# Two-layer FoX/NSA trunk on one core: the z sections of layer 0 three head pairs later

## The chip, the core and the metric

The kernel runs on one core of a Trainium2 chip. The metric is device time in microseconds (us) for one launch. A core has a matrix engine (PE, with its weight loads shown apart as PEld), a vector engine (DVE), a scalar engine (ACT), a general engine (POOL) and a queue engine (SP), which issues all DMAs of this kernel. Each engine works off its own list of instructions in order.

## What is computed

Two layers act on x of 1024 tokens by 1024 channels. Layer 0 is forgetting attention with 16 heads of 64 channels, layer 1 is sparse attention. The change touches layer 0 alone. Cut to that:

```python
h = rmsnorm(x, norm_g[0])
q, k, v, f, z = split(h @ w_in)           # 1024 channels each, f 16
c = cumsum(log_sigmoid(f + b_f))
logits = q k^T / 8 + c[query] - c[key]    # causal, per head
o = softmax(logits) v
x = x + (o * silu(z)) @ w_out
```

## The kernel before, in words

**Units of work.** Heads go in pairs p = 0 to 7; a pair is 128 channels. A *section* is the projection of h to 128 channels of k, v, q or z: two halves of 512 tokens, and for each half eight *triples* (`mm3`, L132 to L135: three matmuls of 512 columns that build one float32 product out of high and low parts). So a section is 16 triples. `load_w` (L123) brings a section's weights by DMA, DVE makes the high part (L128) and POOL the low part (L129); `next_w` loads one section ahead.

**Attention** of a pair is eight *duos* (`FoxDuo`, L538 on). A duo is `score` (S matmuls L579 and L580, three chunks; DVE adds the bias and finds the minimum, L588; ACT exp, L597, and copy, L598; DVE low part, L599; a transposing DMA to `pT`, L600), and, two duos later, `pv` (L613, L614) and `finish` (small DVE work, L622 to L627). After the eighth duo of a pair `finish` transposes the pair's output (`pto`, L635, two groups of four), multiplies it by silu(z) on DVE (L637) and stores it in DRAM as rows of `oF` (L638). The S chunks have three PSUM buffers (`psS`, L50).

**Order.** `merge` (L208) writes the attention (`fox_main`, L653) and the sections (`fox_fill`, L438) into one order: after each step of a duo (its scores, its pv) it takes triples from the fill until their written costs (650 a triple) come up to `ratio` times the written costs of the attention so far. `PACE` is 2.3, and 2.6 (`LAST`) from the eighth pair on. The last triple may overshoot, and with `rebase` an overshoot is not given back. A step may wait for a mark in `ready`: the attention of pair p waits for q of p; k of pair p waits in the fill until all scores of pair p - 2 are written, and v of p until its last `finish`. While the fill waits so, attention steps follow one another without triples, and the triples owed are written in one run when the mark is there. The framework keeps this order on each engine, and draws a later instruction ahead where it reckons that an earlier one would wait.

**Fill.** The sections stand in the order z0 k1 v1 q1 z1 k2 ... (k0 v0 q0 come before the attention). For pair 7 they are split: half of q7, half of z7, `load_wout` of half the output weights (DMA, ACT copy L530, POOL subtraction L531), then the other halves. Behind that stands `out_start` (L464): triples `y` of the output projection of token tiles 4, 5 and 6 with rows 0 to 3, then 4 to 6 of `oF` as far as pairs 0 to 6 go, and row 7 at the end. `out_layer` (L673) does the other five tiles, and layer 1 follows.

Of the kernel before, what the change touches and what calls it, by code (L numbers as in the profile page):

```python
# [8 lines left out]
F32 = mybir.dt.float32  # L9
# [4 lines left out]
AF = mybir.ActivationFunctionType  # L14
OP = mybir.AluOpType
# [4 lines left out]
D = 1024  # L20
S = 1024
P = 128
# [13 lines left out]
def f(ap):  # L36
    return ap.bitcast(F32)
# [3 lines left out]
def tile_fox_nsa(ctx, tc, a, out):  # L41
    nc = tc.nc
    V, A, G, T = nc.vector, nc.scalar, nc.gpsimd, nc.tensor
    dma = nc.sync.dma_start
# [3 lines left out]
    dram = ctx.enter_context(tc.tile_pool(name="dram", bufs=1, space=DRAM))  # L48
# [13 lines left out]
    def ps_a(name):  # L62
        return psA.tile([P, 512], F32, tag="A", name=name)
# [14 lines left out]
    ready = {}  # L78

    def silu2(dst, src):  # L80

        A.activation(dst, src, AF.Tanh, scale=0.5)
        V.scalar_tensor_tensor(dst, dst, 1.0, src, OP.add, OP.mult)
# [168 lines left out]
    oF = dram.tile([D, S], F32, name="oF")  # L252
# [3 lines left out]
    hp = tc.alloc_tile_pool(name="hT0", bufs=1, side="right")  # L256
    st = tc.alloc_tile_pool(name="start", bufs=1, side="right")
    sa = tc.alloc_tile_pool(name="sa", bufs=2)
# [2 lines left out]
    def wsec(kind, p):  # L261
        return load_w(wp, a["fox_w"][kind * 8 + p], f"{'qkvz'[kind]}{p}")

    fox_order = [x for p in range(8) for x in ((1, p), (2, p), (0, p), (3, p))][1:]
    wq = []

    def next_w(take=True):
        while len(wq) < 2 and fox_order:
            wq.append(wsec(*fox_order.pop(0)))
        return wq.pop(0) if take else None  # L270
# [51 lines left out]
    sb = []  # L322
# [94 lines left out]
    def fox_q(p, w, halves=(1, 0)):  # L417
        Q = ready.setdefault(("qt", p), {})
        for half in halves:
            pt = ps_a(f"q{p}_{half}")  # L420
            yield from project(w, hT, half, pt)
            for j in range(2):
                Q[half, j] = q = sa.tile([P, 512], F32R, tag="Q", bufs=8, name=f"Q_{p}_{half}_{j}")
                r, o = rows[j], rows[1 - j]
                A.activation(q[r, :], pt[r, :], AF.Copy, scale=-SCALE)
                V.scalar_tensor_tensor(q[o, :], pt[r, :], -SCALE, f(q[r, :]), OP.mult, OP.subtract)
            ready["q", p, half] = Q

    def fox_z(p, w, halves=(1, 0)):
        zs = ready.setdefault(("zt", p), {})  # L430
        for half in halves:
            pt = ps_a(f"z{p}_{half}")
            yield from project(w, hT, half, pt)
            zs[half] = z = sb[0].tile([P, 512], F32, tag="z", bufs=4, name=f"z_{p}_{half}")
            silu2(z, pt)
            ready["z", p, half] = zs

    def fox_fill():  # L438
        for p in range(8):
            if p >= 2:  # L440
                yield lambda p=p: ("scored", p - 2) in ready
            yield from k0 if p == 0 else fox_k(p)
            if p == 0:
                for _ in range(11):
                    yield next(gate0)
            if p >= 2:
                yield lambda p=p: ("done", p - 2) in ready
            yield from fox_v(p)
            if p == 0:
                yield from gate0  # L450
                sb.append(tc.alloc_tile_pool(name="sb", bufs=2, reuse_waits="tile"))
            wo_copy(0, p)
            if p < 7:
                yield from fox_q(p, next_w())
                yield from fox_z(p, next_w())
            else:
                wq, wz = next_w(), next_w()
                for half in (1, 0):
                    yield from fox_q(p, wq, (half,))
                    yield from fox_z(p, wz, (half,))  # L460
                    yield from load_wout(hp, 0, half)
        yield from out_start()

    def out_start():  # L464


        ys = ready["ys"] = {}
        ws = {}

        def split(t, c, src):  # L470
            oh, ol = ws[t]
            A.copy(oh[:, c, :], src)
            V.tensor_tensor(ol[:, c, :], src, f(oh[:, c, :]), OP.subtract)

        def rows_of(t, c):
            yield lambda: ("o", c.stop - 1, 1) in ready
            of = wp.tile([P, KC, P], F32, tag="wst", bufs=1, name=f"of0{t}_{c.start}")
            dma(of[:, c, :], oF[c.start * P:c.stop * P, t * P:(t + 1) * P].rearrange("(k p) t -> p k t", p=P))
            split(t, c, of[:, c, :])

        def products(t, c):
            oh, ol = ws[t]
            for half in range(2):
                for k in range(c.start, c.stop):
                    wh, wl = ready["wout"][k // 4]
                    cs = slice(half * 512, half * 512 + 512)
                    mm3(ys[t][half], oh[:, k, :], ol[:, k, :], wh[:, k % 4, cs], wl[:, k % 4, cs], k == 0, k == KC - 1)
                    yield 650

        for t, banks in ((4, (ps_a, ps_s)), (5, (ps_a, ps_t))):  # L490
            ws[t] = out_parts(f"0{t}")
            ys[t] = [ps(f"y0_{t}_{half}") for half, ps in enumerate(banks)]
            yield from rows_of(t, slice(0, 4))
            yield from products(t, slice(0, 4))
        for t in (4, 5):
            yield from rows_of(t, slice(4, 7))
        ws[6] = [sa.tile([P, S], F32R, tag=x, bufs=4, name=f"o06_{x}").rearrange("p (k t) -> p k t", k=KC) for x in ("KH", "KL")]
        yield from rows_of(6, slice(0, 7))
        for t in (4, 5):
            yield from products(t, slice(4, 7))  # L500
        yield lambda: "scores" in ready
        ys[6] = [ps_s(f"y0_6_{half}") for half in range(2)]
        yield from products(6, slice(0, 7))
        yield lambda: ("o", 7, 1) in ready
        for t in (4, 5, 6):
            split(t, slice(7, 8), ready["z", 7, 1][1][:, (t - 4) * P:(t - 3) * P].rearrange("p (k t) -> p k t", k=1))
        for t in (4, 5, 6):
            yield from products(t, slice(7, 8))

# [23 lines left out]
        ready.setdefault("wout", []).append((hi, lo))  # L533


    PACE, LAST = 2.3, 2.6

    class FoxDuo:  # L538

# [77 lines left out]
        def finish(self):  # L617
            p, j, x, lr = self.p, self.j, self.x, self.lr
            if j == x == 0:
                self.O[p] = sb[0].tile([P, NT, P], F32, tag="o", bufs=1, name=f"o_{p}")  # L620
            o = self.O[p]
            V.tensor_tensor(lr[:, 1:2], lr[:, 1:2], lr[:, 2:3], OP.add)  # L622
            V.reciprocal(lr[:, 4:6], lr[:, 0:2])
            t = sb[0].tile([P, 2, 64], F32, tag="ot", bufs=2, name=f"ot_{self.name}")
            V.tensor_reduce(t, self.po.rearrange("p (u c) -> p u c", u=2)[:, :, 0:128].rearrange("p u (c d) -> p u d c", c=2),
                            AX.X, OP.add)
            V.tensor_tensor(o[:, 3 - x:5 + x:2 * x + 1, 64 * j:64 * j + 64], t, lr[:, 4:6, None].to_broadcast([P, 2, 64]), OP.mult)  # L627
            if j == 1 and x == 3:
                ready["done", p] = True
                for s in (1, 0):  # L630
                    yield lambda s=s: ("z", p, s) in ready
                    yield 1000
                    pt = ps_t(f"pto_{p}_{s}")
                    for i in range(4):
                        T.transpose(pt[:, i * P:(i + 1) * P], o[:, 4 * s + i, :], ident)  # L635
                    z = ready["z", p, s][s]
                    V.scalar_tensor_tensor(z, pt, ready["v", p][1], z, OP.mult, OP.mult)  # L637
                    dma(oF[p * P:(p + 1) * P, s * 512:(s + 1) * 512], z)  # L638
                    ready["o", p, s] = True
                    yield 450  # L640

    def burst(gens):
# [10 lines left out]
    def fox_main():  # L653
        duos = [FoxDuo(p, j, x) for p in range(8) for j in range(2) for x in range(4)]
        for n in range(len(duos) + 2):
            if n == len(duos) - 8:
                yield (LAST,)
            if n < len(duos):
                yield from burst(duos[n].score(u) for u in (1, 0))
                if duos[n].j == 1 and duos[n].x == 3:  # L660
                    ready["scored", duos[n].p] = True
                    if duos[n].p == 7:
                        ready["scores"] = True
            if n >= 2:
                yield from burst(duos[n - 2].pv(u) for u in (0, 1))
                yield from duos[n - 2].finish()

    merge(fox_main(), fox_fill(), PACE, rebase=True)
    sb[0].release()
    sa.release()  # L670

# [81 lines left out]
    nq, wq = list(nsa_w), []  # L753
# [446 lines left out]
    for qi in range(4):  # L1200
        n = P * (qi + 5)
# [262 lines left out]
```

## Time and profile before

| | us |
|---|---|
| median of 3 runs | 1553.28 |
| those runs | 1551.80 to 1553.96 |
| profiled execution, its time | 1553.53 |
| profiled execution, span from first to last instruction | 1551.7 |

The span is 1.83 us shorter than the time of the same execution. In the rows of stretches further down the columns are: from:to, length in us, busy us of PE, PEld, DVE, ACT and POOL, each with "(x90)" for 90 instructions, then the TensorE clock that was granted (1.00 is 2.4 GHz, 0.50 is 1.2 GHz), the mean busy share of the 16 DMA engines and GB/s. In rows in order of time the first two numbers are start and duration in us. A bracket such as `[2.19 <-DVE m L588]` gives the idle time of the engine before the instruction and what ended it. Layer 0's attention lies between about 72 and 585 us of the span.

### The profile page before, as it was taken

Reading aid. Unit: us, or ns where it says so; the run is one execution under the profiler, and the core shown is the slowest. Engines: PE = TensorE matmul, PEld = TensorE weight load, DVE = VectorE, ACT = ScalarE, POOL = GpSimd, SP = SyncE. Lnnn points to the kernel's source line nnn. Section 1 sums busy time; section 2 is a strip of 40 time slices with the busy share of each in tenths; the row PEclk is TensorE's granted clock in tenths of the full one; section 3 lists DMA queues with packets and bytes.
Section 4 is the critical chain, followed back from the end, with each engine's and each line's share of the span. In section 5 each row is a group of like instructions: output and inputs, shape, how many; then the busy total and the mean of one; then the engine's idle time right before and its main releaser. Section 6 shows DMA issues by size and latency. Waiting matters only on the chain.

```text
span 1551.7 us, 29460 instructions
## 1 busy us (share of the span) xinstructions
PE 1434.4 (92%) x10488; PEld 1188.4 (77%) x10488; DVE 1063.7 (69%) x2756; ACT 803.3 (52%) x2025; POOL 556.5 (36%) x604
## 2 busy tenths in 40 slices
PE   5999999999999787999999979899898998888898
PEld 4888888888787666878888768687787877667686
DVE  6586878778787755457364687787686777678433
ACT  5364646545555643233133655566565666567321
POOL 1232323222233500043241342557647657345300
PEclk9999999999999889999999999999999999899899
DMA  7796767867878756343345586757756856674642
GB/s 263 223 183 146 163 155 156 172 160 149 178 156 174 166 104 231 95 133 96 126 134 176 149 202 179 206 123 151 168 122 143 195 118 137 151 167 113 161 138 95
DMA packets 405763, 242.72 MB, mean 156 GB/s; under 512 B 332464, under 2 KB 353840, under 8 KB 405360
## 3 DMA queue, kind: packets, MB, share of 16 engines
q1 hardware_dynamic: 405616, 240.84, 63.5%
q8 instruction: 83, 1.36, 0.4%
q14 instruction: 64, 0.52, 0.1%
HBM read 120.96 MB, written 44.11 MB: 106 GB/s over the span
## 4 chain that ended last, share of the span: by engine, by line
PE 61%; DVE 16%; ACT 6%; DMA 6%; POOL 6%; issue 4%; SPq 1%; POOLq 0%; DVEq 0%; ACTq 0%
PE S_n L1256 4%; DVE P_n L1263 3%; PE y L133 3%; PE y L135 3%; PE y L134 3%; POOL hl_n L1270 3%; PE ptp_n L1288 2%; PE v L133 2%; PE v L135 2%; PE v L134 2%; PE S L579 2%; PE S L580 2%; PE q L133 2%; PE O L613 2%; PE k L133 2%
## 5 line engine op out<-in xcount | busy, mean ns | idle before, releaser
L1266 ACT ACTIVATE P_n<-P_n,m_n 128x640 f32<-128x640 f32 (+7 forms) x256 | 187.0, 731 | 74.6 <-DVE m_n L1265 37.3
L1256 PE MATMUL S_n<-nk,nq 128*128 128x320 f32 (+5 forms) x768 | 189.0, 356 | 19.4 <-DVE m_n L1263 18.6
L597 ACT ACTIVATE P<-P,m 128x512 f32<-128x512 f32 (+1 forms) x192 | 116.9, 610 | 133.2 <-DVE m L588 132.3
L568 POOL TENSOR_TENSOR Bd<-B,tri 128x128 f32<-128x128 f32 x128 | 62.3, 501 | 245.3 <-DVE m L588 228.5
L1263 DVE CUSTOM_DVE_ANT_0 P_n<-S_n,wmask 128x128 f32<-128x128 f32 (+1 forms) x192 | 113.5, 598 | 53.4 <-POOL hl_n L1270 37.7
L1256 PEld LDWEIGHTS S_n<-nk,nq 128*128 128x128 f32 x768 | 125.2, 194 | 32.3 <-DVE m_n L1263 23.3
L1270 POOL TENSOR_TENSOR hl_n<-P_n,hl_n 128x640 f16<-128x640 f32 (+4 forms) x128 | 141.5, 1109 | 7.5
L599 DVE SCALAR_TENSOR_TENSOR hl<-P,hl 128x512 f16<-128x512 f32 (+1 forms) x192 | 124.1, 664 | 21.8 <-ACT hl L598 20.7
L150 ACT ACTIVATE pth_n<-ptp_n 128x512 f16<-128x512 f32 (+1 forms) x160 | 86.6, 546 | 76.1 <-PE ptp_n L1288 75.4
L1288 PE MATMUL ptp_n<-ident,P_n 128*128 128x128 f32 x576 | 98.2, 292 | 19.3 <-DVE ptl_n L151 10.3
L151 DVE SCALAR_TENSOR_TENSOR ptl_n<-ptp_n,pth_n 128x512 f16<-128x512 f32 (+1 forms) x160 | 100.5, 634 | 20.8 <-ACT pth_n L150 20.1
L1269 POOL CAST hl_n<-P_n 128x640 f16<-128x640 f32 (+4 forms) x128 | 74.1, 584 | 98.7 <-ACT P_n L1266 78.4
L133 PE MATMUL y<-wo,ohi 128*128 128x512 f32 x240 | 96.8, 403 | 8.0 <-ACT ohi L693 8.0
L1288 PEld LDWEIGHTS ptp_n<-ident,P_n 128*128 128x128 f32 x576 | 71.3, 149 | 33.1 <-DVE ptl_n L151 11.9
L134 PE MATMUL y<-wo,ohi 128*128 128x512 f32 x240 | 96.0, 400 | 0.0
L135 PE MATMUL y<-wo,olo 128*128 128x512 f32 x240 | 94.9, 398 | 0.9 <-DVE olo L694 0.9
L598 ACT ACTIVATE hl<-P 128x512 f16<-128x512 f32 (+1 forms) x192 | 92.5, 513 | 4.3 <-DMA pT<-hl 2.8
L1296 PE MATMUL O_n<-nv,pth_n 128*128 128x64 f16 x576 | 76.1, 199 | 3.7 <-ACT pth_n L150 3.7
L579 PE MATMUL S<-KH,Q 128*128 128x512 f32 (+1 forms) x192 | 68.8, 372 | 10.6 <-DVE m L588 10.4
L1297 PE MATMUL O_n<-nv,pth_n 128*128 128x64 f16 x576 | 74.9, 197 | 0.0
L1298 PE MATMUL O_n<-nv,ptl_n 128*128 128x64 f16 x576 | 72.2, 197 | 0.0
L1296 PEld LDWEIGHTS <-pth_n 128*128 128x128 f16 x576 | 53.8, 101 | 21.4 <-ACT pth_n L150 9.1
(384 smaller groups left out, 4517.0 us busy)
## 6 DMA issues: line engine op xcount, KB each, us to landing
nq<-qD SPq DMA_DIRECT2D x64, 256.0 KB
B<-cD SPq DMA_DIRECT2D x16, 512.0 KB
wo<-wD SPq DMA_DIRECT2D x16, 512.0 KB
nq<-qD SPq DMA_DIRECT2D x64, 128.0 KB
of<-oF SPq DMA_DIRECT2D x12, 512.0 KB
x<-in_x_dram SPq DMA_DIRECT2D x8, 512.0 KB
wst_k<-in_fox_w_dram SPq DMA_DIRECT2D x8, 512.0 KB
wst_v<-in_fox_w_dram SPq DMA_DIRECT2D x8, 512.0 KB
```

The costliest lines, as they stand in the source:

```text
L133: T.matmul(ps, wh, mh, start=first, stop=False, **kw)
L134: T.matmul(ps, wh, ml, start=False, stop=False, **kw)
L135: T.matmul(ps, wl, mh, start=False, stop=last, **kw)
L151: V.scalar_tensor_tensor(lo[:, 0:n], pt[:, 0:n], scale, h, OP.mult, OP.subtract)
L597: A.activation(L[:, 0:n], L[:, 0:n], AF.Exp, bias=init, scale=-1.0, accum_out=self.lr[:, col + c:col + c + 1])
L599: V.scalar_tensor_tensor(lo[:, cs], L[:, 0:n], UP, hi[:, cs], OP.mult, OP.subtract)
L1256: T.matmul(ps[:, b, 0:w], self.q[x][:, qi * P:(qi + 1) * P], k[:, k0 + b * w:k0 + b * w + w], start=(x == 0), stop=(x == 1))
L1263: V.tensor_tensor_reduce(dst, src, mk, 1.0, 3e38, OP.add, OP.min, m)
L1266: A.activation(L, L, AF.Exp, bias=m, scale=-1.0, accum_out=self.l[:, y, qi:qi + 1])
L1270: G.tensor_tensor(hl[:, n:2 * n], L, hl[:, 0:n], OP.subtract)
L1288: T.transpose(pt[:, (x + i) * P:(x + i + 1) * P], L[:, kb * P - k0:(kb + 1) * P - k0], ident)
L1296: T.matmul(o, hi, v[:, 0:64], start=first, stop=False)
```

## The change

The z section of a pair is computed three pairs later: z0 follows q3, and so on; z5, z6 and z7 stand behind q7, z6 and z7 by halves, with `load_wout` behind each half. Since a pair's output is then ready before its z, `finish` no longer multiplies for pairs 0 to 6: ACT scales the transposed output into a tile, and a DMA stores it in a new DRAM tensor `oZ`. `fox_z` loads it back, computes silu(z), lets POOL multiply, and stores the rows of `oF`. Pair 7 stays as it was, with its z in another buffer. The pace is 1.75 (`FIRST`) for the first two pairs, then 2.3, and 2.6 as before for the last.

```diff
@@ -261,7 +261,9 @@
     def wsec(kind, p):
         return load_w(wp, a["fox_w"][kind * 8 + p], f"{'qkvz'[kind]}{p}")
 
-    fox_order = [x for p in range(8) for x in ((1, p), (2, p), (0, p), (3, p))][1:]
+    DZ = 3
+    fox_order = [x for p in range(8) for x in ((1, p), (2, p), (0, p)) + (((3, p - DZ),) if p >= DZ else ())]
+    fox_order = (fox_order + [(3, p) for p in range(8 - DZ, 8)])[1:]
     wq = []
 
     def next_w(take=True):
@@ -426,14 +428,28 @@
                 V.scalar_tensor_tensor(q[o, :], pt[r, :], -SCALE, f(q[r, :]), OP.mult, OP.subtract)
             ready["q", p, half] = Q
 
+    oZ = dram.tile([D, S], F32, name="oZ")
+
     def fox_z(p, w, halves=(1, 0)):
-        zs = ready.setdefault(("zt", p), {})
+
         for half in halves:
+            r, c = slice(p * P, (p + 1) * P), slice(half * 512, half * 512 + 512)
+            if p < 7:
+                yield lambda half=half: ("oz", p, half) in ready
+                o = sb[0].tile([P, 512], F32, tag="z", bufs=4, name=f"oz_{p}_{half}")
+                dma(o, oZ[r, c])
             pt = ps_a(f"z{p}_{half}")
             yield from project(w, hT, half, pt)
-            zs[half] = z = sb[0].tile([P, 512], F32, tag="z", bufs=4, name=f"z_{p}_{half}")
-            silu2(z, pt)
-            ready["z", p, half] = zs
+            if p < 7:
+                z = sb[0].tile([P, 512], F32, tag="z", bufs=4, name=f"z_{p}_{half}")
+                silu2(z, pt)
+                G.tensor_tensor(z, z, o, OP.mult)
+                dma(oF[r, c], z)
+                ready["o", p, half] = True
+            else:
+                z = sa.tile([P, 512], F32, tag="vs", bufs=2, name=f"z_{p}_{half}")
+                silu2(z, pt)
+                ready["z", p, half] = z
 
     def fox_fill():
         for p in range(8):
@@ -450,15 +466,16 @@
                 yield from gate0
                 sb.append(tc.alloc_tile_pool(name="sb", bufs=2, reuse_waits="tile"))
             wo_copy(0, p)
-            if p < 7:
-                yield from fox_q(p, next_w())
-                yield from fox_z(p, next_w())
-            else:
-                wq, wz = next_w(), next_w()
-                for half in (1, 0):
-                    yield from fox_q(p, wq, (half,))
-                    yield from fox_z(p, wz, (half,))
-                    yield from load_wout(hp, 0, half)
+            yield from fox_q(p, next_w())
+            if p >= DZ:
+                yield from fox_z(p - DZ, next_w())
+        for p in range(8 - DZ, 6):
+            yield from fox_z(p, next_w())
+        ws = [next_w(), next_w()]
+        for half in (1, 0):
+            for p in (6, 7):
+                yield from fox_z(p, ws[p - 6], (half,))
+            yield from load_wout(hp, 0, half)
         yield from out_start()
 
     def out_start():
@@ -503,7 +520,7 @@
         yield from products(6, slice(0, 7))
         yield lambda: ("o", 7, 1) in ready
         for t in (4, 5, 6):
-            split(t, slice(7, 8), ready["z", 7, 1][1][:, (t - 4) * P:(t - 3) * P].rearrange("p (k t) -> p k t", k=1))
+            split(t, slice(7, 8), ready["z", 7, 1][:, (t - 4) * P:(t - 3) * P].rearrange("p (k t) -> p k t", k=1))
         for t in (4, 5, 6):
             yield from products(t, slice(7, 8))
 
@@ -533,7 +550,7 @@
         ready.setdefault("wout", []).append((hi, lo))
 
 
-    PACE, LAST = 2.3, 2.6
+    FIRST, PACE, LAST = 1.75, 2.3, 2.6
 
     class FoxDuo:
 
@@ -628,15 +645,23 @@
             if j == 1 and x == 3:
                 ready["done", p] = True
                 for s in (1, 0):
-                    yield lambda s=s: ("z", p, s) in ready
+                    if p == 7:
+                        yield lambda s=s: ("z", p, s) in ready
                     yield 1000
                     pt = ps_t(f"pto_{p}_{s}")
                     for i in range(4):
                         T.transpose(pt[:, i * P:(i + 1) * P], o[:, 4 * s + i, :], ident)
-                    z = ready["z", p, s][s]
-                    V.scalar_tensor_tensor(z, pt, ready["v", p][1], z, OP.mult, OP.mult)
-                    dma(oF[p * P:(p + 1) * P, s * 512:(s + 1) * 512], z)
-                    ready["o", p, s] = True
+                    r, c = slice(p * P, (p + 1) * P), slice(s * 512, s * 512 + 512)
+                    if p < 7:
+                        z = sb[0].tile([P, 512], F32, tag="z", bufs=4, name=f"ov_{p}_{s}")
+                        A.activation(z, pt, AF.Copy, scale=ready["v", p][1])
+                        dma(oZ[r, c], z)
+                        ready["oz", p, s] = True
+                    else:
+                        z = ready["z", p, s]
+                        V.scalar_tensor_tensor(z, pt, ready["v", p][1], z, OP.mult, OP.mult)
+                        dma(oF[r, c], z)
+                        ready["o", p, s] = True
                     yield 450
 
     def burst(gens):
@@ -653,6 +678,8 @@
     def fox_main():
         duos = [FoxDuo(p, j, x) for p in range(8) for j in range(2) for x in range(4)]
         for n in range(len(duos) + 2):
+            if n == 8 * (DZ - 1):
+                yield (PACE,)
             if n == len(duos) - 8:
                 yield (LAST,)
             if n < len(duos):
@@ -665,7 +692,7 @@
                 yield from burst(duos[n - 2].pv(u) for u in (0, 1))
                 yield from duos[n - 2].finish()
 
-    merge(fox_main(), fox_fill(), PACE, rebase=True)
+    merge(fox_main(), fox_fill(), FIRST, rebase=True)
     sb[0].release()
     sa.release()
 
```

## Rows read from the trace of the kernel before

**Rows 1.** The page: busy engines, then PE and its clock in 40 slices of the span.

```profile
PE 1434.4 (92%) x10488; PEld 1188.4 (77%) x10488; DVE 1063.7 (69%) x2756; ACT 803.3 (52%) x2025; POOL 556.5 (36%) x604
...
PE   5999999999999787999999979899898998888898
...
PEclk9999999999999889999999999999999999899899
```

**Rows 2.** Stretches: pairs 0 and 3, then pair 7's first S to the late y.

```profile
71.62:129.80 58.18, 58.18 (x350) 47.74 (x349) 46.48 (x146) 37.06 (x92) 20.64 (x25) 1.00 0.86 175
...
256.25:319.52 63.27, 63.27 (x405) 52.26 (x404) 48.85 (x156) 38.36 (x96) 17.36 (x20) 1.00 0.81 169
...
514.95:569.12 54.17, 39.69 (x265) 31.07 (x264) 38.33 (x130) 32.32 (x85) 15.85 (x20) 0.84 0.73 146
```

**Rows 3.** Waits of PE from 495 to 640 us: total, times, longest.

```profile
PE S L579 <- DVE m L588: 10.4, 9, 2.8
```

**Rows 4.** PE in order of time: start, us; sixteen triples between these two rows.

```profile
117.20 0.47 PE L133 MATMUL q<-hT,whi_q 128*128 128x512 f32 x1
...
128.21 0.39 PE L133 MATMUL z<-hT,whi_z 128*128 128x512 f32 x1
```

**Rows 5.** PE in order of time: the first S chunks of two neighbouring duos.

```profile
299.27 0.34 PE L579 MATMUL S<-KH,Q 128*128 128x384 f32 x1
...
305.99 0.28 PE L579 MATMUL S<-KH,Q 128*128 128x256 f32 x1
```

**Rows 6.** PE in order of time: the scores of pair 6's last duo.

```profile
504.71 0.44 PE L579 MATMUL S<-KH,Q 128*128 128x128 f32 x1 [2.19 <-DVE m L588]
```

**Rows 7.** Two stretches of 5 us behind that wait (columns as in rows 2).

```profile
505.00:510.00 5.00, 4.94 (x13) 3.40 (x13) 4.87 (x11) 4.67 (x12) 3.92 (x5) 0.50 0.51 101
510.00:515.00 5.00, 5.00 (x35) 4.00 (x34) 4.11 (x14) 1.90 (x6) 1.69 (x3) 0.86 0.99 216
```

**Rows 8.** PE in time: last S chunk of pair 7's last three duos.

```profile
556.94 0.77 PE L579 MATMUL S<-KH,Q 128*128 128x512 f32 x1 [0.53 <-DVE m L588]
...
561.27 0.78 PE L579 MATMUL S<-KH,Q 128*128 128x512 f32 x1
...
564.86 0.51 PE L579 MATMUL S<-KH,Q 128*128 128x512 f32 x1 [0.81 <-DVE m L588]
```

**Rows 9.** Groups by line, 71 to 500 us: busy us, mean ns | idle before.

```profile
L637 DVE SCALAR_TENSOR_TENSOR z<-pto,vsc,z 128x512 f32<-128x512 f32 x12 | 9.0, 748 | 10.0 <-PE pto L635 9.9
...
L83 DVE SCALAR_TENSOR_TENSOR z<-z,z 128x512 f32<-128x512 f32 x15 | 10.2, 683 | 0.6 <-ACT z L82 0.3
...
L82 ACT ACTIVATE z<-z 128x512 f32<-128x512 f32 x15 | 8.9, 593 | 4.7 <-PE z L135 4.6
...
L128 DVE CAST whi_z<-wst_z 128x1024 fp32r<-128x1024 f32 x7 | 5.0, 717 | 0.7 <-PE v L134 0.7
...
L129 POOL TENSOR_TENSOR wlo_z<-wst_z,whi_z 128x1024 fp32r<-128x1024 f32 x7 | 17.3, 2471 | 17.8 <-issue 4.8 <-PE S L580 4.8 <-DVE vsc L173 4.4
```

**Rows 10.** POOL and DVE in order of time, one moment.

```profile
308.85 2.39 POOL L129 TENSOR_TENSOR wlo_k<-wst_k,whi_k 128x1024 fp32r<-128x1024 f32 x1
...
304.77 1.02 DVE L599 SCALAR_TENSOR_TENSOR hl<-P,hl 128x256 f16<-128x256 f32 x2
...
309.16 2.37 DVE L599 SCALAR_TENSOR_TENSOR hl<-P,hl 128x256 f16<-128x256 f32 x1
```

**Rows 11.** The 20 us with the busiest DVE of the steady part.

```profile
440.00:460.00 20.00, 20.00 (x135) 16.50 (x134) 17.95 (x52) 12.04 (x32) 6.43 (x8) 1.00 0.81 177
```

**Rows 12.** PE in time: pair 7's S drawn between pair 6's output transposes.

```profile
529.57 0.49 PE L635 MATMUL pto<-ident,o 128*128 128x128 f32 x3
529.82 0.37 PE L579 MATMUL S<-KH,Q 128*128 128x256 f32 x1
```

**Rows 13.** The chain that ended last: a store of `oF` (start, us).

```profile
584.88 2.04 DMA oF<-z
```

## The prediction

> **What bounds the kernel now.** I read the page first: PE is busy 92% of the span, and its slices say where it is not: full up to about 500 us, then a dip in which its clock falls too [rows 1]. The second view splits layer 0's attention by head pairs. In pair 3 PE is busy 63.27 of 63.27 us at full clock, while DVE has 48.85 us, 77% [rows 2]: PE's own work sets the time there, and a section more or less in that stretch is worth what PE needs for it. From the first S of pair 7 (514.95 us) to the first late `y` (569.12 us; late: it waits for all scores) PE is busy 39.69 us of 54.17, at a clock of 0.84 [rows 2]. The waits say why: the S matmuls wait for DVE's minima (10.4 us in nine waits [rows 3]). Eight duos stand there with few triples between them, so DVE's chain is all there is. Work of PE that needs nothing of pair 7 would fit, and the z sections are such work. The remaining views price the pieces: the order of PE in time, and the groups by line.
>
> **Prices on PE.** Sixteen triples, one section, take 128.21 - 117.20 = 11.01 us, so a triple takes 0.688 us [rows 4]. Two neighbouring duos start 6.72 us apart with seven triples between them [rows 5]: a duo costs PE 6.72 - 7 x 0.688 = 1.90 us.
>
> **Where the triples land.** I went through `merge`'s rule with the costs written in the code; for the kernel before this gives three and four triples in turn between the steps of a duo, as the seven of rows 5 show. In the new order it gives six triples a duo in pairs 0 and 1 and seven after that, so q3 is reached early, and z5 ends just ahead of pair 7's first scores. So up to those scores PE has 30 sections behind it instead of 32, and no `y` (before: seven triples). Between them and the late `y` stand z6 and z7 (32 triples) and the 28 triples `y` of tiles 4 and 5.
>
> **Step 1, up to pair 7's first S.** PE loses 39 triples, 26.8 us. The stall of 2.19 us at 504.71 us [rows 6] and the slow clock behind it (0.50 for 4.94 busy us, then 0.86: 2.5 + 0.7 us [rows 7]) came where scores met the weight split of `load_wout` on POOL and no z was left; in the new order z5 stands there. I take these 5.4 us as gone. First S of pair 7: 514.95 [rows 2] - 32.2 = 482.7 us, before the losses of step 3.
>
> **Step 2, pair 7.** Work of PE from its first S to the late `y`: eight duos 15.2, 60 triples 41.3, the transposes of pair 6 0.7; 57.2 us. By the count the last two duos still have no triples beside them, because the late `y` waits for all scores. Such bare duos took 561.27 - 556.94 = 4.33 and 564.86 - 561.27 = 3.59 us before [rows 8], mean 3.96, so 2 x 2.06 = 4.1 us are idle. From the last chunk (564.86 [rows 8]) to the late `y` 4.26 us passed; 0.8 us of pv is in the 57.2 already, 3.5 us I leave in. Sum 64.8 us against 54.17, so the late `y` starts at 547.5 instead of 569.12 us: -21.6 us. DVE's 38.3 us [rows 2] and the four silu products of 0.68 us [rows 9] fit in 64.8. The tail behind stays: row 7 of `oF` and its round trip are untouched [rows 13].
>
> **Step 3, what it costs earlier.** Pairs 0 and 1: a duo with six triples is 6.03 us of PE. DVE's 48.85 us of a pair [rows 2] lose silu (2 x 0.68), one weight cast (0.72) and the final products (2 x 0.75 [rows 9]): 45.3 us, 5.7 us a duo, 94% of PE's. The busiest steady 20 us had DVE at 17.95, 90%, with PE full [rows 11], so it is just beyond what is seen. Between 0 and 8 us (0.5 us in each of 16 duos); I take 2, as it is nearer to rows 11 than to a full DVE.
>
> Bare steps: by the same count the new fill runs into its own marks from pair 1 on. k of a pair waits for all scores two pairs earlier, v for their last `finish`; z used to stand between q and the next k and gave slack. I count 34 steps of duos without triples ahead of pair 7's first S, against two before, in ten runs of two to four steps, and five more at pair 7's start, where z6 waits for pair 6's output; the triples owed follow in runs of 11 to 17 us. At worst each of these 20 duos idles 2.06 us: 41 us. At best none: the order draws ready work ahead of a waiting instruction, as S of pair 7 between the transposes of pair 6 [rows 12], and the next k or v needs only its weights and a PSUM buffer. I take 5 us, 0.45 us a run, near the lower end, because of rows 12.
>
> The new operations: 14 copies on ACT in place of 14 DVE products of 0.75 us; a like ACT pass over z takes 0.59 us [rows 9]; ACT is busy 61% of a pair [rows 2]. Hidden; if not, 8 us. DVE gives back 10.5 us. POOL gets 14 products of 512 columns, half of the 2.47 us of 1024 columns [rows 9]: 1.24 us each, queued ahead of the bias tiles (L568) that scores need. One row shows what DVE pays beside such a product: a low part of 256 columns took 2.37 us, two of them 1.02 us elsewhere [rows 10]. So 14 x 1.24 = 17.4 us of DVE at most, 7 us net of the 10.5. Hidden in pairs 2 to 7, where DVE has 20% to spare; I take 0.
>
> The DMAs: 14 stores to `oZ` and 14 loads more, all on SP, with the transposing DMAs of L600 queued behind them. A store of this size took 2.04 us to land [rows 13]; the load after it is three pairs late except for pair 6, where SP may hold the next transposes for some 2 us; pv follows two duos, 12 us, after its scores. Zero; if uncovered, 2 us for each half of pair 6. In pair 0 the DMA engines are at 0.86 already [rows 2], and the pair gets 11 us shorter less one weight load; that belongs to the 0 to 8 us above.
>
> **Sum.** -21.6 + 2 + 5 = -14.6 us against the profiled 1553.53 (span 1551.7 and 1.83 around it), which lies 0.25 above the median: **1538.9 us**, 0.94% faster.
>
> **A rule against the change.** DVE waits for POOL's product in rows 10. The Trainium skill, GPSIMD Engine Reference, sections 4.1 and 8, puts products of two tensors on the vector engine, with POOL about twice as slow and sharing its SBUF interfaces with DVE. The trace agrees: 1.24 us by rows 9 against 0.68. The rival "DVE pays" is what follows if that share lies on the path.
>
> **The rivals.** *DVE pays*: pairs 2 to 7 have too little slack, each of the 14 products costs the path its 7 us net, or ACT's copies delay exp: 1539 + 7 = 1546 us. For it: DVE at 90% in rows 11. Against: PE never waited there. *Bare runs fall short (slower)*: nothing is drawn ahead, because the next k or v finds no PSUM buffer, and every bare duo idles its 2.06 us: -21.6 + 2 + 41 = +21 us, 1575 us; with a slow clock after each run, as after 504.71 (3.2 us), more. It decides from 20 us on, 1 us a duo, half of the full price. For it: waits of 2 us did halve the clock [rows 6, 7]. Against: rows 12. In the Trainium skill, TensorE: Matmul & The Clock Gate, section HAM oscillation, a loop pays the slow clock anew at each gap; rows 6 and 7 agree for one gap, and no row shows ten. *It does not do what it says*: pair 7's gaps take no work, since DVE's chain is held up by as much as z adds (its silu, ACT's tanh, the weight split that now follows z7 and that `y` waits for); the 39 triples that step 1 takes away, 26.8 us, then lengthen this stretch by as much, and only the 5.4 us are gained: -5.4 + 7, 1555 us. Against: neither PE nor DVE is full there [rows 2]. *Better*: no loss in step 3 and a last pair without its slow end, -25 us, 1528 us.
>
> **How the numbers follow.** Forecast (-10 to -21 us) 0.50; DVE pays (-3.1 to -10) 0.14; better 0.12; no change that a measurement can tell, within 0.2% or 3.1 us, 0.10, half of it the third rival; slower 0.14, most of it bare runs. So faster 0.76, same 0.10, slower 0.14. Range 1529 (the better case's near half) to 1555, which leaves out about 0.05 below and 0.14 above.
>
> **What would show it.** Right: first S of pair 7 near 490 us, the late `y` near 554, PE full from 72 to about 550 with clock 1.00, few waits of S for DVE ahead of pair 7. Wrong: waits of S for DVE of more than 15 us between 120 and 490 us, a clock below 0.97 there, or a distance from pair 7's first S to the late `y` of over 72 us.

## The result, and the profile after

The changed kernel takes 1564.94 us (median of 5 runs, 1562.98 to 1571.11) against 1552.98 us (5 runs, 1549.75 to 1553.96) before: ratio 1.0089, interval 1.0065 to 1.0114. It is slower by 0.9%, where 0.94% faster was forecast; the time lies outside the range. The profiled execution is the longest of the five, 1571.11 us with a span of 1569.3.

The page of the changed kernel, PE's busy share and granted clock in 40 slices of 39.2 us, answers to [rows 1]:

```profile
PE 1437.1 (92%) x10488; PEld 1190.5 (76%) x10488; DVE 1057.8 (67%) x2742; ACT 811.9 (52%) x2039; POOL 576.5 (37%) x618
...
PE   5999999998989878999999898899898998888898
...
PEclk9999999999999999999999999999999999989899
```

In PE's row the one dip before layer 1 has become several; the clock's row hides them, since a 9 is 90% or more. The stretches of the same trace (columns as in [rows 2]): first S to pair 7's first S, then to the late `y`; before, these were 71.62 to 514.95 and 514.95 to 569.12 us. Below them pairs 3 and 4 alone.

```profile
72.00:511.40 439.40, 419.62 (x2646) 343.65 (x2646) 339.29 (x1037) 255.16 (x636) 135.85 (x154) 0.98 0.78 170
511.40:590.64 79.24, 63.76 (x386) 50.65 (x383) 46.13 (x135) 40.91 (x100) 35.10 (x32) 0.91 0.66 159
...
242.13:309.47 67.34, 63.87 (x399) 52.23 (x398) 50.47 (x155) 38.82 (x96) 19.96 (x22) 0.97 0.80 167
309.47:380.48 71.01, 65.37 (x399) 53.17 (x398) 50.41 (x152) 37.83 (x93) 19.27 (x22) 0.95 0.81 168
```

Pair 7's first S came at 511.40 us, only 3.6 us earlier: the 39 triples (26.8 us) had gone from ahead of it, but 19.78 us of idle time (439.40 - 419.62) and a slowed clock took most of their place. Pair 4 is 71.01 us long with 5.64 idle; in the kernel before it had none. Pair 7 itself took 79.24 us, 15.48 of them idle. So the late `y` starts at 590.64 us, 21.5 later than before. From there to the end of the span it is 978.7 us here, 982.6 in the profile before, and 974.8 to 982.5 in the profiles of the eleven runs below: what lies behind scatters by 8 us from execution to execution, so places in layer 0 are compared by their own start, and whole times by medians, 12.0 us apart.

The waits of PE in the long stretch, in the changed kernel (total, times, longest), then the longest of them in order of time, rows of several engines:

```profile
PE O L630 <- DMA pT<-hl: 9.8, 8, 2.4
PE S L596 <- DVE m L605: 6.0, 2, 4.2
PE v L133 <- DVE ot L642: 2.4, 2, 1.5
PE k L133 <- DVE z L83: 1.3, 1, 1.3
```

```profile
429.62 0.39 PE L596 MATMUL S<-KH,Q 128*128 128x512 f32 x1
...
430.16 2.35 POOL L129 TENSOR_TENSOR wlo_v<-wst_v,whi_v 128x1024 fp32r<-128x1024 f32 x1 [1.67 <-PE S L597]
430.39 2.40 DVE L616 SCALAR_TENSOR_TENSOR hl<-P,hl 128x256 f16<-128x256 f32 x1
...
432.79 0.40 DVE L642 TENSOR_REDUCE ot<-O 128x128 f32<-128x256 f32 x1
...
433.71 0.68 DVE L83 SCALAR_TENSOR_TENSOR z<-z,z 128x512 f32<-128x512 f32 x1
...
435.56 0.45 PE L596 MATMUL S<-KH,Q 128*128 128x128 f32 x1 [4.20 <-DVE m L605]
...
435.61 0.41 DVE L642 TENSOR_REDUCE ot<-O 128x128 f32<-128x256 f32 x1
...
439.95 0.72 PE L133 MATMUL k<-hT,whi_k 128*128 128x512 f32 x1
```

This is one of the runs of steps without triples that the prediction counted: z3's last triples, two duos bare, then k7's sixteen triples in one run from 439.95 us. S stands first in PE's list and waits 4.20 us for DVE; k7 stands behind, and no triple of it was drawn ahead. DVE is late because one of its steps ran 2.40 us beside POOL's product.

For part of that wait k7 could not have run either. A section needs a PSUM buffer, and sections and pv share three (`psA`, L51). From 430.42 us, when the last pv ahead of the wait begins, all three are held: by z3's last half until L83 has read it (433.71 + 0.68), and by two duos' outputs until L642 has reduced them (433.19 and 436.02 us). So in the first 1.8 us of the wait no buffer was free, and the same late DVE step held them. The last two lines of waits are this case seen directly: a v or a k at the head of the list waits for DVE to give a buffer free, 3.7 us in three waits. The largest item, 9.8 us, is pv waiting for its transposes.

What the long wait does to the clock, in the same execution:

```profile
430.00:435.00 5.00, 1.19 (x20) 0.79 (x18) 4.79 (x11) 1.36 (x4) 2.89 (x2) 0.87 0.47 116
435.00:440.00 5.00, 4.44 (x27) 3.58 (x27) 4.78 (x22) 4.30 (x13) 2.48 (x5) 0.50 0.86 188
```

The granted clock is 0.50 in the 5 us behind the gap: the wait is paid again in a slow clock, as in [rows 6, 7]. How often that happens differs between executions (a2_again below).

### The profile page after: what moved, and what is told of

It reads as the page before. It is cut to its first block, busy times and chain, and to the rows that moved or that the text cites. A ratio compares the mean times of both kernels' runs of the same rounds, so it can differ in the third digit from the quotient of the medians.

```text
span 1569.3 us, 29530 instructions
## 1 busy us (share of the span) xinstructions
PE 1437.1 (92%) x10488; PEld 1190.5 (76%) x10488; DVE 1057.8 (67%) x2742; ACT 811.9 (52%) x2039; POOL 576.5 (37%) x618
## 5 line engine op out<-in xcount | busy, mean ns | idle before, releaser
L596 PE MATMUL S<-KH,Q 128*128 128x512 f32 (+1 forms) x192 | 68.4, 371 | 14.5 <-DVE m L605 14.3
L630 PEld LDWEIGHTS <-pT 128*128 128x128 f16 x576 | 51.1, 101 | 28.6 <-DMA pT<-hl 15.1
```

## The experiments

Two theories stood against each other. M: the fill runs into its own marks, and steps without triples make the loss. N: the new operations do (POOL's products hold DVE, SP waits for them). Ratios are to the kernel before, run on the same chip beside each group.

| run | what | us | ratio, interval | first S of pair 7 | late y |
|---|---|---|---|---|---|
| a2_again | the changed kernel | 1565.97 | 1.0068, 1.0048 to 1.0088 | 506.1 | 585.1 |
| e1_pace | paces 1.5, 2.0 | 1543.40 | 0.9920, 0.9891 to 0.9949 | 481.1 | 563.4 |
| e4_half | paces 1.75, 2.0 | 1549.61 | 0.9972, 0.9959 to 0.9985 | 483.1 | 567.6 |
| e7_oldpace | before, pace 2.0 | 1572.17 | 1.0119, 1.0094 to 1.0144 | 532.5 | 590.7 |
| e2_ops | before, new operations | 1552.31 | 0.9978, 0.9959 to 0.9996 | 514.6 | 569.2 |
| e3_dve | products on DVE | 1561.97 | 1.0048, 1.0027 to 1.0069 | 503.5 | 579.4 |
| e9_lowdve | weights' low part on DVE | 1561.23 | 1.0037, 1.0019 to 1.0054 | 498.8 | 576.9 |
| e5_split | e1, `load_wout` split on DVE | 1541.88 | 0.9907, 0.9876 to 0.9939 | 478.8 | 560.8 |
| e8_dveall | e5, products on DVE | 1541.20 | 0.9899, 0.9883 to 0.9914 | 481.1 | 563.1 |
| e6_two | z two pairs later, 1.75, 2.0 | 1544.64 | 0.9928, 0.9905 to 0.9952 | 486.1 | 561.4 |
| e11_twosplit | e6, split on DVE | 1544.23 | 0.9937, 0.9912 to 0.9961 | 489.2 | 567.5 |

The last two columns are us from the start of each run's profiled span.

**The marks: e1_pace.** A lower pace, so that the fill does not reach its marks.

```diff
-    FIRST, PACE, LAST = 1.75, 2.3, 2.6
+    FIRST, PACE, LAST = 1.5, 2.0, 2.6
```

> Only the pace is changed: 1.5 for the first two pairs (was 1.75), 2.0 for the next five (was 2.3). By a count of merge's rule no step of a duo ahead of pair 7 is then without triples (34 in the changed kernel); 14 more triples of z come to stand beside pair 7. Theory M (the marks: steps without triples idle PE and slow its clock; the changed kernel's trace has 19.8 us idle and about 11 us of slow clock between the first S and pair 7's first S): those 30 us go, about 1540 us, 1535 to 1547. Theory N (the new operations: POOL's products hold DVE, SP waits for them): they are all still there, 1560 to 1566 us.

Measured 1543.40 us, 22.6 less than the changed kernel beside it (a2_again) and 0.8% faster than before. Theory M holds, N does not. The profile of e1_pace, first S to pair 7's first S, and from there to the late `y`:

```profile
70.89:481.12 410.23, 403.87 (x2605) 331.88 (x2605) 325.74 (x1036) 258.28 (x639) 130.63 (x151) 0.99 0.84 179
481.12:563.43 82.31, 73.17 (x423) 58.54 (x422) 51.38 (x140) 41.43 (x100) 38.33 (x35) 0.94 0.70 174
```

Pairs 3 to 6 take 60.56 us each with no idle time; the 6.36 us that are left lie in pairs 0 and 1. All new operations are still there. The lower pace also moves 14 triples (9.6 us) behind pair 7's first S. With these added back, e1_pace's profile gains 15.3 us on a2_again's ahead of that S (481.1 + 9.6 against 506.1) and another 6.3 us from there to the late `y`, where the moved triples fill idle time and the wait at pair 7's start is 2.3 us instead of 4.1. So not all of the 22.6 us is the price of the steps ahead of pair 7.

**A dose: e4_half.** Only the middle pace lowered; by `merge`'s rule the fill then stands at a mark after nine steps, instead of after 34.

```diff
-    FIRST, PACE, LAST = 1.75, 2.3, 2.6
+    FIRST, PACE, LAST = 1.75, 2.0, 2.6
```

> Only the pace of pairs 2 to 6 is changed, 2.0 instead of 2.3; 1.75 stays for the first two. By the count 9 steps ahead of pair 7's first S are without triples (34 in the changed kernel at 1566 us, none in e1_pace at 1543.4). Theory M, each such step costs about the same (22.6 us / 34 = 0.66 us): 1549 us, 1546 to 1552. Rival (the pace of the first two pairs makes the loss): above 1556.

Measured 1549.61 us: with 34, 9 and 0 such steps the times are 1566, 1549.6 and 1543.4, so more of them cost more. One price for all is not shown. A step at a mark still gets the triples that come before the mark: in PE's order in the traces 22, 3 and 0 of the 110 steps (scores or pv) ahead of pair 7's first S have no triple before the next. By the first count a step costs 0.65 us from e4_half to the changed kernel and 0.69 from e1_pace to e4_half; by the second it is 0.86 and 2.1. Both take the whole time, pair 7 included.

**Is it the pace alone? e7_oldpace.** The kernel before at the lower pace.

```diff
-    PACE, LAST = 2.3, 2.6
+    PACE, LAST = 2.0, 2.6
```

> The kernel before with its pace at 2.0 instead of 2.3 and nothing else. By the count 35 triples then stand between pair 7's first S and the late y (21 before, 74 in e1_pace). Theory Z, e1_pace owes its gain to the moved z sections: 1549 to 1554. Rival P, the pace alone does it: 1542 to 1546.

Measured 1572.17 us, slower than any other: neither expectation holds, and rival P is out. With z between q and the next k, the lower pace has q ready too late when its pair begins. PE's waits between 60 and 640 us in e7_oldpace, and one of them in order of time, with DVE:

```profile
PE S L579 <- DVE Q L426: 19.5, 6, 3.9
...
259.69 3.43 DVE L599 SCALAR_TENSOR_TENSOR hl<-P,hl 128x512 f16<-128x512 f32 x2
263.15 0.68 DVE L426 SCALAR_TENSOR_TENSOR Q<-q,Q 64x512 fp32r<-64x512 f32 x1
...
263.89 0.79 PE L579 MATMUL S<-KH,Q 128*128 128x512 f32 x1 [3.67 <-DVE Q L426]
```

q's last triple ends 2.5 us before PE turns to the scores (8.0 us in the kernel before, at the same pair), and the scores wait for q's copy, which stands behind two low parts on DVE: 3.6 to 3.9 us at the start of each of pairs 2 to 6. So a pace has two sides, and moving z shifts the balance between them.

**The new operations alone: e2_ops.** The order of before; in `finish`, for pairs 0 to 6 (the tensor `oZ` and a fifth buffer of tag `z` are not shown):

```diff
-                    V.scalar_tensor_tensor(z, pt, ready["v", p][1], z, OP.mult, OP.mult)
-                    dma(oF[p * P:(p + 1) * P, s * 512:(s + 1) * 512], z)
+                        ov = sb[0].tile([P, 512], F32, tag="z", bufs=5, name=f"ov_{p}_{s}")
+                        A.activation(ov, pt, AF.Copy, scale=ready["v", p][1])
+                        dma(oZ[r, c], ov)
+                        G.tensor_tensor(z, z, ov, OP.mult)
+                        dma(oF[r, c], z)
+                        if p:
+                            dma(ov, oZ[(p - 1) * P:p * P, c])
```

> The kernel before in its own order, with the new operations of pairs 0 to 6: ACT scales the transposed output, a store to oZ, POOL multiplies by silu(z), a load of the same size from oZ (of the pair before, not used). Theory M: within 2 us of the kernel before, 1551 to 1555. Theory N: the loss of the changed kernel, 1558 to 1565.

Measured 1552.31 us, not slower than before. In this order, ACT's copies, POOL's products and the DMAs are hidden.

**The products on DVE: e3_dve.**

```diff
-                G.tensor_tensor(z, z, o, OP.mult)
+                V.tensor_tensor(z, z, o, OP.mult)
```

> The changed kernel with its 14 products on DVE instead of POOL. Theory M: pairs 0 to 6 as they are; pair 7 gains up to 5 us, since there SP's store waits for a product behind the weight split on POOL: 1559 to 1566 us. Theory N: most of the loss goes, 1550 to 1556 us.

Measured 1561.97 us, 4.0 less than a2_again, with intervals that overlap; as M expected. What it shows is in its trace. In the changed kernel the longest wait beside pair 7 has this chain: SP, POOL, ACT, DVE, PE in order of time.

```profile
552.85 1.72 POOL L446 TENSOR_TENSOR z<-z,oz 128x512 f32<-128x512 f32 x1
...
554.60 0.33 SPq L447 DMA_DIRECT2D oF<-z  x1
555.02 0.37 SPq L543 DMA_DIRECT2D wo<-wD  x1
...
560.86 1.14 ACT L547 CAST wo<-wo 128x512 fp32r<-128x512 f32 x2 [5.74 <-DMA wo<-wD]
...
563.45 0.61 DVE L639 TENSOR_TENSOR l<-l 128x1 f32<-128x1 f32 x1 [6.67 <-ACT P L614]
...
566.19 0.80 PE L596 MATMUL S<-KH,Q 128*128 128x512 f32 x1 [7.50 <-DVE m L605]
```

SP's store of z6 waits for a product that stands on POOL behind the weight split; the loads of the output weights stand behind the store; ACT's exps stand behind the copies of those weights. In e3_dve the loads start at 544.80 us, 41.3 us behind pair 7's first S instead of 43.6, and the same S (554.14 us there) waits 1.21 us:

```profile
554.14 0.50 PE L596 MATMUL S<-KH,Q 128*128 128x512 f32 x1 [1.21 <-DVE m L605]
```

Beside pair 7 PE idles 11.53 us there, against 15.48 in the changed kernel: part of what this wait lost comes back as other waits.

**POOL's low part beside the bare steps: e9_lowdve.** In `load_w`:

```diff
-        G.tensor_tensor(lo, st, f(hi), OP.subtract)
+        V.tensor_tensor(lo, st, f(hi), OP.subtract)
```

> The changed kernel (paces 1.75 and 2.3, 34 steps without triples) with load_w's low part of the weights on DVE instead of POOL. Theory W, a step without triples is long because POOL's low part of the next weights holds DVE just there (in the changed kernel's trace a step of DVE of 0.5 us took 2.40 beside it): 8 us or more less than the changed kernel, below 1558. Rival B (DVE's chain is as long by itself, as in pair 7 before, and 4 more us of DVE a pair make it longer): 1563 to 1572.

Measured 1561.23 us, some 5 us less than a2_again by the two ratios: less of a gain than theory W asked, more than rival B allowed. Pair 4 still idles 2.96 us and pair 5 4.87 (5.64 and 5.84 in the changed kernel). POOL's hold on DVE is part of a bare step's price; more than half stays without it, with the low part now on DVE (8.4 us idle in pairs 3 to 5, against 14.4 in a2_again).

**Beside pair 7: e5_split and e8_dveall.** e1_pace with the weight split of `load_wout` on DVE, then with the edit of e3_dve too.

```diff
-                (V if i else G).tensor_tensor(lo[:, k, cs], f(lo[:, k, cs]), f(hi[:, k, cs]), OP.subtract)
+                V.tensor_tensor(lo[:, k, cs], f(lo[:, k, cs]), f(hi[:, k, cs]), OP.subtract)
```

> e1_pace with the weight split of load_wout (16 subtractions) on DVE instead of POOL. Theory H, POOL's two-tensor products hold DVE's small steps beside pair 7 (in e1_pace's trace a step of 0.28 us took 1.39 and 2.11 us): 3 to 6 us less than e1_pace, 1537 to 1540. Rival (DVE is short of time there, whoever splits): 1543 to 1548.

> e5_split (paces 1.5 and 2.0, weight split of load_wout on DVE) with the 14 products on DVE too. Theory H, every product taken off POOL frees DVE's small steps and SP's store beside pair 7: 1 to 4 us less than e5_split, 1538 to 1541. Rival (DVE's own added 10 us of products cost as much): 1541 to 1545.

Measured 1541.88 and 1541.20 us against 1543.40: in the direction of theory H, but the intervals lie over one another. e8_dveall has the lowest ratio of all, 0.9899, 1% faster than before; how much of its lead over e1_pace is real stays open.

**The first pairs: e6_two and e11_twosplit.** `DZ = 2`, paces 1.75 and 2.0; then the edit of e5_split too.

```diff
-    DZ = 3
+    DZ = 2
-    FIRST, PACE, LAST = 1.75, 2.3, 2.6
+    FIRST, PACE, LAST = 1.75, 2.0, 2.6
```

> z two pairs later instead of three, paces 1.75 (first pair) and 2.0: no step without triples either, and only pair 0 is without z, so DVE has more PE time in pair 1. Theory D, DVE is short in pairs 0 and 1 (e1_pace's trace: 5.6 us of PE idle there and a slow clock in one slice): 3 us less than e1_pace, 1539 to 1542. Rival (those waits come from the transposing DMAs and stay): 1543 to 1546.

> e6_two (z two pairs later, paces 1.75 and 2.0) with the weight split of load_wout on DVE. Theory H: 3 us less than e6_two, 1540 to 1543. Rival: 1544 to 1548.

Measured 1544.64 and 1544.23 us: no gain over e1_pace. Pair 1 has no idle time in e6_two (1.91 us in e1_pace), pair 0 keeps 2.36, and pair 7 idles more (13.93 against 9.14 us). Theory D holds for pair 1 and is worth about 2 us there.

**Repeat: a2_again.** The changed kernel, unchanged.

> The changed kernel again, for a second trace beside the others on the same chip: 1563 to 1571 us by both theories.

Measured 1565.97 us; late `y` at 585.07 us, 5.6 earlier than in the first profile, with the same idle times by pair within 0.7 us. What differs is the clock. The long stretch, pairs 3 and 4, and the 5 us behind the same wait of S (4.10 us here):

```profile
72.29:506.09 433.80, 414.47 (x2646) 339.84 (x2646) 338.85 (x1037) 255.07 (x636) 135.72 (x154) 0.99 0.80 172
...
242.64:307.70 65.06, 62.28 (x399) 51.09 (x398) 50.45 (x155) 38.82 (x96) 19.98 (x22) 1.00 0.81 173
307.70:375.98 68.28, 62.55 (x400) 51.16 (x398) 50.35 (x152) 37.83 (x93) 19.25 (x22) 1.00 0.84 172
...
431.00:436.00 5.00, 4.93 (x31) 3.90 (x32) 4.78 (x19) 4.75 (x15) 1.99 (x5) 0.67 0.85 163
```

Pairs 3 and 4 kept the full clock behind waits after which it fell in the first profile (0.97 and 0.95). So the idle time of the bare steps is steady, and what the clock adds to it is not.

## Why the prediction was wrong

**What bounds the kernel: right.** PE's own work set the time of pairs 0 to 6, and work without bearing on pair 7 fits beside it. In e1_pace pair 7's first S came at 481.1 us with 14 triples more moved behind it; with their 9.6 us that is 490.7, and without its 6.36 us of idle time 484.4, against 482.7 forecast ahead of any loss. So step 1 holds once the bare steps are gone, and the late `y` comes 5.7 us earlier than before. One reading was off: of the 10.4 us in rows 3, 2.2 are the wait of rows 6, ahead of pair 7; its own waits for the minima are 8.2 us of 14.5 idle.

**Where the triples land: right, but for the count of bare steps.** The order in the trace is the counted one: z5 ends at 510.8 us, just ahead of pair 7's scores. The 34 steps are those at which the fill runs into a mark; 22 of the 110 have no triple at all in the trace.

**Step 3, the bare steps: the term that failed.** It was put at 5 us between 0 and 41, on the ground that the order draws ready work ahead [rows 12]. It drew none of the triples: at 435.56 us S has waited 4.20 us with sixteen of them behind it, for which no PSUM buffer was free in the first 1.8 us at least. In the changed kernel pairs 3 to 5 idle 14.95 us and the slow clock (0.97, 0.95 and 0.96 over 67, 71 and 57 us) takes some 8 more; in a2_again it is 14.35 and about 1. So the term measured 15 to 23 us, and the 15.3 us that e1_pace wins back ahead of pair 7 agree. Rows 12 showed pair 7's scores drawn over transposes that waited, one wait among short steps; they said nothing of a fill behind a whole run of bare steps, nor of the buffers that it needs, and they should not have carried the choice near the lower end. The duos of 3.6 to 4.3 us in [rows 8] were the row that fitted: at 2.06 us a duo, 1.03 a step, the 22 steps come to 22.7 us, the upper end of what was measured.

The rival "bare runs fall short" named the mechanism, gave 1575 us and most of the 0.14 for slower, and put its turning point at 20 us. Measured: 15 to 23 us ahead of pair 7's first S, and a wait of 4.1 us at pair 7's start. Its condition, no PSUM buffer for the next k or v, is seen in three waits (3.7 us) and in the start of the longest one. Whether a free buffer would have brought triples ahead was not tested, so how much of the loss it explains stays open; shown is that no triple was drawn ahead.

**Step 3, the first pairs:** 2 us were taken of 0 to 8. The changed kernel idles 4.84 us in pairs 0 and 1, with a clock of 0.97 in pair 0 (1.6 us): 6 us, inside the bounds. The waits there are for transposes on their way (`pT`, 2.35 us at 102.84 us), not for the minima: SP stands 4.4 us at one transposing DMA from 95.48 us, for DVE, with the next ones behind it.

**Step 2, pair 7: 64.8 us forecast, 79.24 measured.** The triples were right. Idle time was put at 7.6 us with the clock's share; it was 15.48 plus 0.09 x 79.24 = 7.1 us. Two waits make the surplus: 4.08 us where z6 waits for its mark at pair 7's start, a bare run again, and the 7.50 us of the chain above. In PE's waits from pair 7's first S to the late `y` (total, times, longest) they are:

```profile
PE S L596 <- DVE m L605: 8.3, 2, 7.5
PE pto L653 <- DVE o L644: 4.1, 1, 4.1
```

For that chain the prediction had written "SP may hold the next transposes for some 2 us" and taken zero; the price was right for a store that lands, but the store here waits for POOL, and what it held were the output weights, not transposes.

**The new operations: right at zero in pairs 0 to 6, in the order of before** (e2_ops); in the new order that store beside pair 7 is the exception. The rival "DVE pays" asked 7 us of the products; on DVE instead they gave back 4.0 us, with intervals that overlap (e3_dve). The rule of the Trainium skill, GPSIMD Engine Reference, section 4.1, puts such products on the vector engine; following it was worth these 4.0 us here, if that, and e3_dve is still slower than before.

**Sum:** 14.6 us earlier were forecast for the late `y`, 21.5 later came in the first profile: 36.1 us. Of these, 22 are the losses up to pair 7's first S (29 against 7) and 14 pair 7. In a2_again the late `y` is 16.0 us later than before, and the sum 30.6 us.

## What to carry to other kernels

A hand-written interleave has marks that the filling work waits for, and moving a section out of its place also moves the slack that it gave them: count the steps that then run without cover, and retune the pace with the move (here 22.6 us, from 0.7% slower to 0.8% faster). A lower pace is no remedy by itself: without the move it cost 1.2%, because the next pair's input then came late. When an engine's list is in order, price an uncovered step by a bare step that the trace already shows, and take no credit for reordering unless the trace shows it in the same situation, with a buffer free for the work that is to be drawn ahead.

## What the hardware showed

A two-tensor product on POOL holds a step of DVE whose two tensors both lie in SBUF until the product ends, however small the step is: 0.28 us became 2.11 beside a 2.34 us weight product, and a step of one column went from 0.16 to 1.23 beside the split of `load_wout`, both in e1_pace. Steps that read PSUM kept their length there: the minima of 512 columns (L605) took 0.75 us with such a product running and without. In order of time, in e1_pace:

```profile
496.75 2.34 POOL L129 TENSOR_TENSOR wlo_z<-wst_z,whi_z 128x1024 fp32r<-128x1024 f32 x1 [3.59 <-issue]
...
497.13 2.11 DVE L644 TENSOR_TENSOR o<-ot,l 128x128 f32<-128x128 f32 x1
...
543.19 5.24 POOL L548 TENSOR_TENSOR wo<-wo,wo 128x512 fp32r<-128x512 f32 x4
...
546.00 1.23 DVE L639 TENSOR_TENSOR l<-l 128x1 f32<-128x1 f32 x1
```

The prices on DVE and POOL by group means hide this, since most instances run free; it falls where POOL's products crowd, which is beside pair 7 and at the marks, where the next weights are split.
